# A two-layer decoder step on one core: raw tokens in column pieces as first operands, the norm's factor applied to the projections' outputs, and the samples' sums and recurrence in other steps

## The chip, the core and the metric

The kernel runs on one core of a Trainium2 chip. Five engines work at the same time, each through its own instructions in order: TensorE (PE; its weight loads are shown apart as PEld), VectorE (DVE), ScalarE (ACT), GpSimd (POOL) and SyncE (SP), which here only issues transfers. The metric is the device time of one execution in microseconds (us). Times of before are a median of three runs; the profile is of one further execution.

## The reference

One inference step of a decoder with a prompt of 1024 tokens and 8 single-token samples that share all weights (width 1024, FFN width 2816, fp32). Layer A mixes with a gated linear recurrence (4 heads, a 128x128 state each) beside attention over 256 memory tokens, layer B with stick-breaking attention beside memory attention; each is followed by a SwiGLU FFN. Every sub-layer has a norm before and behind it. What the change touches, in short:

```python
def rmsnorm(x, g):
    y = xf * lax.rsqrt(jnp.mean(xf * xf, axis=-1, keepdims=True) + EPS)
    return (y * g.astype(jnp.float32)).astype(x.dtype)
def a_mixer(hn, w_in, lb, hg_gain, mem_k, mem_v, w_o, s0):      # hn = rmsnorm(h, g[0])
    q_h, f_h, i_h, g_h, q_m = jnp.split(hn @ w_in, 5, axis=-1)
    q = jax.nn.silu(q_h)                       # logf, k from f_h; v = i_h
    o, S = hgrn2_scan(q, k, v, logf, s0)       # S <- exp(logf) * S + k v,  o = q S
    o = rmsnorm(o, hg_gain) * jax.nn.silu(g_h)
    om = mem_attend(q_m, mem_k, mem_v)         # softmax(q k / sqrt(d)) v
    return jnp.concatenate([o, om], axis=-1) @ w_o, S
```

Since `hn @ w_in` is linear, a token's factor 1/rms can be applied to a projection's output as well as to its input.

## The kernel before

The prompt is worked on in two groups of 512 tokens (g = 0 and 1); the 8 samples ride with group 1, whose rows are 520 wide. Activations lie with the features across partitions, eight blocks of 128 (`ND` = 8). Every fp32 operand is split in two fp32r tiles, a high part (a cast on ScalarE) and the remainder (a subtraction on VectorE, `split_to` and the pair L208/L209 for weights), and every product is three matmuls (high by high, high by low, low by high). TensorE therefore has 24 matmuls of 512 columns for a projection of one head (`proj`, L222), and the FFN's gate and up projections are partly done with Strassen's seven products (`gate_up_w`; L571, L573 split its weights, L578 is its product).

**The start.** `start(0)` waits for four blocks of 128 tokens by 1024 features, norms each (`rms_rows`: squares at L331 or L333, Ln and Exp, multiplication L336), turns them feature by feature on TensorE (L363, four transposes for one block of 128 features) and multiplies by the norm's gain while it splits (L366 on ScalarE, L367 on VectorE). The first projection is that of the values, token rows out (`rows_proj`, L1183: for each of eight feature blocks, twelve matmuls in two pairs of banks), whose weights are cast at L1177 and L1178 and whose result is copied at L1189 and L1190. The gate's projection (`gate_proj`) follows, L222 again, then q.

**The samples' recurrence.** `hgrn_sample` goes through four heads: a state tile and the values of one head, copied to all partitions, are fetched one head ahead (L1248, from the input and from `vd`). On VectorE the state is multiplied by F (L1272), the values by K (L1273), they are added (L1274), and stored (L1275); the next step multiplies by Q (L1278) and splits for TensorE. It is woven with the second group's gate projections and with the FFN of group 0.

**The samples' memory attention.** `mem_attn_sample` has `sample_scores` and `sample_pv`, which for each sample loads its cached values, multiplies and adds them on VectorE, splits them, and sums over partitions on TensorE (L1071 into one bank); the result is copied (L1091), turned (L1095) and split. It is woven with the prompt's memory attention (L978 turns the probabilities, L991 multiplies by the values) and with the FFN, first an ordinary part (L504 is Strassen's product in it) and then the part with L571 to L578.

**What sets the order.** The program is written with generators that `weave` mixes: each stream has a weight, and the stream with the smallest count of steps over its weight goes next, so a weight decides between which products a step's instructions fall. `tc.issue_after(split[0].ins)` puts an instruction behind the last weight split. Within an engine the order of instructions is that of the program so laid out. PSUM has three banks with tag `s` (`S()`), one with tag `ns` (`NS()`) and four for products.

## Time and profile before

| | |
|---|---|
| three runs | 2410.87 us median (2408.98 to 2412.88) |
| the profiled execution | 2413.43 us |
| its span, first to last instruction | 2411.6 us, mean clock 0.998 |
| VectorE, ScalarE, by 40 us from 40 to 200 | 28.7, 34.5, 30.1, 19.8 and 27.0, 18.5, 17.3, 25.9 us |
| TensorE in the first 40 us | 29.2 us, later 40.0 of 40 |

Lines of the profile read: start and duration in us, engine, source line, operation, tile written, tiles read, how many; in brackets how long the engine had been idle and what released it. A row with "x84" stands for a run of 84 instructions. Rows of SP with the letter q show when a transfer was issued, not when it landed. A windows row gives the stretch, then each engine's busy time with its count, then the granted clock (1 is full), the share of time the DMA engines were busy, and GB/s.

### The profile page before, as it was taken

The page shows a single profiled execution, that of the slowest core. Times are in us where ns is not written, and L with a number is a line of the kernel's source. Part 1 is how long each engine was busy: PE and PEld are TensorE (multiplying, and loading weights), DVE is VectorE, ACT ScalarE, POOL GpSimd, SP SyncE. Part 2 cuts the span into 40 slices and gives each one's busy share as a digit, 9 for nine tenths or more (in the row PEclk, how much of TensorE's full clock was granted, in tenths as well). Part 3 has the DMA queues.
Part 4 walks back from the last instruction along what each step waited for, and adds up shares of the span by engine and source line. Part 5 has one row for each costly group of instructions (what it writes and reads, how often), then busy time and mean ns, then how long its engine had stood idle before and what let it go on. Part 6 is the DMA issues. An engine that isn't in the chain of part 4 may idle for free.

```text
span 2411.6 us, 42315 instructions
## 1 busy us (share of the span) xinstructions
PE 2379.0 (99%) x15959; PEld 2156.3 (89%) x15959; DVE 1734.8 (72%) x3220; ACT 1283.5 (53%) x2559; POOL 113.2 (5%) x187
## 2 busy tenths in 40 slices
PE   8999999999999999999999999999999999999998
PEld 6888989888789998999999989877778899999998
DVE  5867558666896676879666777778787679776866
ACT  5547544444454554667544554556454466554445
POOL 1000202100000000000001200111000000000000
PEclk9999999999999999999999999999999999999999
DMA  6454766566644447432568846545353354343342
GB/s 189 123 167 111 173 194 163 132 187 181 203 140 136 146 139 217 124 112 81 163 176 218 230 141 190 173 137 157 109 157 118 99 160 136 105 130 100 109 128 76
DMA packets 510991, 357.59 MB, mean 148 GB/s; under 512 B 20109, under 2 KB 459514, under 8 KB 510786
## 3 DMA queue, kind: packets, MB, share of 16 engines
q1 hardware_dynamic: 494914, 312.93, 43.6%
q0 software_dynamic: 15872, 41.95, 7.5%
q8 instruction: 126, 2.06, 0.4%
q14 instruction: 79, 0.65, 0.1%
HBM read 322.86 MB, written 65.49 MB: 161 GB/s over the span
## 4 chain that ended last, share of the span: by engine, by line
PE 51%; DVE 2%; ACT 2%; DMA 1%; issue 1%; DVEq 0%; SPq 0%; ACTq 0%
PE mm L222 17%; PE q L578 16%; PE q L750 10%; PE q L504 1%; PE s L1565 1%; PE s L1525 1%; PE q L782 1%; PE s L1010 1%; PE s L991 1%; PE s L1554 1%; DMA w<-in_w_in_b 0%; DVE x L230 0%; PE ns L1071 0%; PE s L978 0%; PE s L504 0%
## 5 line engine op out<-in xcount | busy, mean ns | idle before, releaser
L222 PE MATMUL mm<-x,ws 128*128 128x512 f32 (+1 forms) x5016 | 925.5, 342 | 5.3 <-DVE ws L209 1.5
L222 PEld LDWEIGHTS mm<-x,ws 128*128 128x128 f32 x5016 | 774.5, 188 | 115.9 <-issue 3.9
L208 ACT CAST ws<-w 128x512 fp32r<-128x512 f32 x596 | 347.9, 585 | 435.5 <-PE mm L222 254.4
L209 DVE TENSOR_TENSOR ws<-w,ws 128x512 fp32r<-128x512 f32 x596 | 380.9, 645 | 227.2 <-ACT ws L208 224.2
L750 PE MATMUL q<-m,ws 128*128 128x260 f32 (+1 forms) x2496 | 304.2, 282 | 0.4 <-DVE m L230 0.2
L750 PEld LDWEIGHTS q<-m,ws 128*128 128x128 f32 x2496 | 299.7, 188 | 1.6 <-ACT m L229 0.7
L578 PE MATMUL q<-y,ws 128*128 128x260 f32 (+1 forms) x1920 | 249.6, 284 | 0.5 <-ACT q L586 0.5
L578 PEld LDWEIGHTS q<-y,ws 128*128 128x128 f32 x1920 | 237.8, 189 | 1.6 <-ACT q L586 0.7
L578 PE MATMUL q<-x,ws 128*128 128x260 f32 (+1 forms) x1668 | 220.4, 283 | 3.0 <-ACT ws L571 1.6
L578 PEld LDWEIGHTS q<-x,ws 128*128 128x128 f32 x1668 | 207.8, 188 | 4.4 <-ACT ws L571 2.2
L222 PE MATMUL mm<-m,ws 128*128 128x512 f32 x768 | 187.2, 397 | 0.0
L571 ACT CAST ws<-w 128x512 fp32r<-128x512 f32 x206 | 125.1, 619 | 96.3 <-PE q L750 30.7
L573 DVE TENSOR_TENSOR ws<-w,ws 128x512 fp32r<-128x512 f32 x206 | 139.5, 688 | 44.7 <-ACT ws L571 43.4
L222 PEld LDWEIGHTS mm<-m,ws 128*128 128x128 f32 x768 | 142.5, 188 | 31.3
L759 DVE TENSOR_TENSOR r<-r,q 128x260 f32<-128x260 f32 (+1 forms) x160 | 60.6, 420 | 48.7 <-PE q L750 48.6
L504 PE MATMUL q<-x,ws 128*128 128x260 f32 (+1 forms) x720 | 87.1, 282 | 0.0
L504 PEld LDWEIGHTS q<-x,ws 128*128 128x128 f32 x720 | 86.4, 188 | 0.2
L229 ACT CAST m<-t 128x512 fp32r<-128x512 f32 (+1 forms) x88 | 54.8, 623 | 49.0 <-DVE t L819 26.9
L571 ACT CAST ws<-b 128x512 fp32r<-128x512 f32 x82 | 50.5, 620 | 39.2 <-PE q L750 13.4
L573 DVE TENSOR_TENSOR ws<-b,ws 128x512 fp32r<-128x512 f32 x82 | 56.4, 688 | 17.8 <-ACT ws L571 15.9
L230 DVE TENSOR_TENSOR m<-t,m 128x512 fp32r<-128x512 f32 (+1 forms) x88 | 60.8, 691 | 11.2 <-ACT m L229 10.4
L277 DVE TENSOR_TENSOR st<-st,n 128x512 f32<-128x512 f32 (+1 forms) x91 | 62.2, 691 | 4.0 <-ACT n L276 2.7
(410 smaller groups left out, 3092.0 us busy)
## 6 DMA issues: line engine op xcount, KB each, us to landing
w<-in_w_gu SPq DMA_DIRECT2D x275, 256.0 KB, 3.3
w<-in_w_down SPq DMA_DIRECT2D x160, 256.0 KB, 3.0
wsum<-in_w_gu POOLq DMA_DIRECT2D x48, 512.0 KB, 6.0
w<-in_w_in_a SPq DMA_DIRECT2D x80, 256.0 KB, 3.0
w<-in_w_o SPq DMA_DIRECT2D x64, 256.0 KB, 3.0
w<-wsum SPq DMA_DIRECT2D x61, 256.0 KB, 3.1
b<-in_w_gu SPq DMA_DIRECT2D x39, 256.0 KB, 4.0
b<-wsum SPq DMA_DIRECT2D x39, 256.0 KB, 3.3
```

Of the source, the lines that this page charges most:

```text
L208: nc.scalar.copy(ws[:, 0, :n, :], raw[:, :n, :])
L209: split[0] = nc.vector.tensor_sub(ws[:, 1, :n, :], raw[:, :n, :], ws[:, 0, :n, :].bitcast(F32))
L222: nc.tensor.matmul(ps[:, a, : PW[g]], wt, xt[k][:, xi, o : o + PW[g]], start=(k == 0 and wi == 0), stop=(k == nk - 1 and wi == 2),)
L229: nc.scalar.copy(dst[0], src)
L230: nc.vector.tensor_sub(dst[1], src, dst[0].bitcast(F32))
L277: nc.vector.tensor_add(acc[:, :n], acc[:, :n], t[:, :n])
L504: ins = nc.tensor.matmul(pp[a][:, :h], wt, xt[k][:, xi, a * h : (a + 1) * h], start=(k == 0 and wi == 0), stop=(k == ND - 1 and wi == 2),)
L571: nc.scalar.copy(w[:, 0, :], src)
L573: split[0] = nc.vector.tensor_sub(w[:, 1, :], src, w[:, 0, :].bitcast(F32))
L578: nc.tensor.matmul(ps[:, :h], w[:, wj, k * P : (k + 1) * P], x[:, xi, :], start=(first and k == 0 and wi == 0), stop=(k == 3 and wi == 2), ...
L750: nc.tensor.matmul(pp[a][:, :h], wt, mids[k][:, xi, a * h : (a + 1) * h], start=(k == 0 and wi == 0), stop=(k == nf - 1 and wi == 2),)
L759: nc.vector.tensor_add(d, d, pp[a][:, :h])
```

## The change

**Start.** The tokens of group 0 come in eight pieces of 128 features by 512 tokens, between them the first five blocks of the values' weights. Only the gains of the norms are loaded before them. Transposes and first operands are made of the raw tokens times the gain; their instructions and the products are tied to alternate (`turned`, `summed`). The factors (`token_scales`) are computed later: squares, Ln, Exp, a diagonal, and a product of ones with it, that lays the 512 factors across all partitions (`rows`). Values get the factor of their token when they are copied out, q, gate and memory query by a multiplication with `rows` on VectorE; for the f gate and the memory query this takes the place of a copy on ScalarE. The masks are cast once instead of seven times.

**Samples.** Some small transposes and sums that used the three banks `s` use the bank `ns`. In the recurrence a step ends behind the multiplication by F, and the two following multiplications stand behind the last weight split. Two weights of `weave` are others: 16 for 12 and 70 for 82.

The diff, cut:

```diff
     xtok = [rpool.tile([P, CH, D], F32, tag="r", name="xtok0")]
-    for tb in range(CH):
-        nc.sync.dma_start(xtok[0][:, tb, :], x_prompt[0, tb * P : (tb + 1) * P, :])
     prow = tpool.tile([P, P], F32, tag="t", name="prow")
-    nc.vector.memset(prow, 0.0)
     nc.sync.dma_start(prow[0:NR, :], g_norm.rearrange("l i (k p) -> (l i k) p", p=P))
-    nc.sync.dma_start(prow[NR : NR + ND, :], g_kv.rearrange("(k p) -> k p", p=P))
-    nc.sync.dma_start(prow[NR + ND : NR + ND + H, :], hg_lb.rearrange("l (h p) -> (l h) p", p=P))
-    nc.sync.dma_start(prow[NR + ND + H : NR + ND + H + 1, :], hg_norm)
+    wfirst = []
+    for k in range(ND):
+        cs = slice(k * P, (k + 1) * P)
+        nc.sync.dma_start(xtok[0][:, :, cs], x_prompt[0, :G, cs].rearrange("(c p) d -> p c d", p=P))
+        if k < 5:
+            wfirst.append(wraw.tile([P, 512], F32, tag="w", name=nm("w")))
+            nc.sync.dma_start(wfirst[k], w_in_a[0][cs, 8 * P : 12 * P])
+    prest = tpool.tile([P, P], F32, tag="t", name="prest")
+    nc.sync.dma_start(prest[0:ND, :], g_kv.rearrange("(k p) -> k p", p=P))
+    nc.sync.dma_start(prest[ND : ND + H, :], hg_lb.rearrange("l (h p) -> (l h) p", p=P))
+    nc.sync.dma_start(prest[ND + H : ND + H + 1, :], hg_norm)
...
-    def silu(dst, ps, g):
+    def silu(dst, ps, g, scale=None):
         n = NG[g]
         x = T()
         dst = T() if dst is None else dst
         d = dst[:, :n]
-        nc.vector.tensor_scalar(sv(x, g), pv(ps, g), -44.0, None, op0=ALU.max)
+        src = pv(ps, g)
+        if scale is not None:
+            nc.vector.tensor_mul(sv(x, g), src, scale)
+            src = sv(x, g)
+        nc.vector.tensor_scalar(sv(x, g), src, -44.0, None, op0=ALU.max)
...
+    def token_scales(out):
+        ss = small([P, 8], tag="rr")
+        for tb in range(CH):
+            xt = xtok[0][:, tb, :]
+            junk = M().rearrange("p a n -> p (a n)")[:, :D]
+            with tc.issue_after(turned[-1][tb % 2]):
+                if tb % 2:
+                    nc.vector.tensor_tensor_reduce(junk, xt, xt, 1.0, 0.0, ALU.mult, ALU.add, ss[:, tb : tb + 1])
+                else:
+                    nc.scalar.activation(junk, xt, AF.Square, accum_out=ss[:, tb : tb + 1])
+        nc.scalar.activation(ss[:, :CH], ss[:, :CH], AF.Ln, scale=1.0 / D, bias=epsb)
+        nc.scalar.activation(ss[:, :CH], ss[:, :CH], AF.Exp, scale=-0.5)
+        d = B()
+        nc.vector.tensor_mul(
+            d.rearrange("p (c t) -> p c t", c=CH), ident.unsqueeze(1).to_broadcast([P, CH, P]),
+            ss[:, :CH].unsqueeze(2).to_broadcast([P, CH, P]),
+        )
+        ps = S()
+        nc.tensor.matmul(ps, ones, d, start=True, stop=True)
+        rows = M()[:, 0, :G]
+        nc.scalar.copy(rows, ps)
+        out.extend((ss, rows))
...
             ps = S() if k % 2 else NS()
-            for tb in range(CH):
-                nc.tensor.transpose(ps[:, tb * P : (tb + 1) * P], xtok[g][:, tb, k * P : (k + 1) * P], ident)
+            with ExitStack() as tied:
+                if summed[0] and not g:
+                    tied.enter_context(tc.issue_after(summed[0].ins))
+                for tb in range(CH):
+                    nc.tensor.transpose(ps[:, tb * P : (tb + 1) * P], xtok[g][:, tb, k * P : (k + 1) * P], ident)
             x = X(g)
             gk = gcol(0, 0, k)
-            nc.scalar.activation(x[:, 0, :G], ps, AF.Copy, scale=gk)
+            raised = nc.scalar.activation(x[:, 0, :G], ps, AF.Copy, scale=gk)
...
+            if not g:
+                turned.append((raised.ins, made[0].ins))
...
-        pq = S()
+        pq = NS()
...
-    def rows_proj(W, m0, xt, dst):
+    def rows_proj(W, m0, xt, dst, raws=(), scale=None):
         pb = [mmp.tile([P, 2, 512], F32, tag="mm", name=nm("mm")) for _ in range(2)]
         for k in range(ND):
-            raw = wraw.tile([P, 512], F32, tag="w", name=nm("w"))
-            nc.sync.dma_start(raw, W[k * P : (k + 1) * P, m0 : m0 + H * P])
+            if k < len(raws):
+                raw = raws[k]
+            else:
+                raw = wraw.tile([P, 512], F32, tag="w", name=nm("w"))
+                nc.sync.dma_start(raw, W[k * P : (k + 1) * P, m0 : m0 + H * P])
             ws = wspl.tile([P, 2, 512], F32R, tag="ws", name=nm("ws"))
-            nc.scalar.copy(ws[:, 0, :], raw)
-            nc.vector.tensor_sub(ws[:, 1, :], raw, ws[:, 0, :].bitcast(F32))
+            with ExitStack() as tied:
+                if raws:
+                    tied.enter_context(tc.issue_after(turned[k][0]))
+                nc.scalar.copy(ws[:, 0, :], raw)
+            with ExitStack() as tied:
+                if raws:
+                    tied.enter_context(tc.issue_after(turned[k][1]))
+                nc.vector.tensor_sub(ws[:, 1, :], raw, ws[:, 0, :].bitcast(F32))
...
+                        summed[0] = nc.tensor.matmul(
...
-            if k % 2:
+            if k % 2 or raws:
                 yield
-        nc.scalar.copy(dst[0][:, :, :512], pb[0])
-        nc.vector.tensor_copy(dst[1][:, :, :512], pb[1])
-    def v_proj(g, W, m0, xt, vt, vs):
+        if scale is None:
+            nc.scalar.copy(dst[0][:, :, :512], pb[0])
+            nc.vector.tensor_copy(dst[1][:, :, :512], pb[1])
+            return
+        for a in range(2):
+            nc.scalar.activation(dst[0][:, a, :512], pb[0][:, a, :], AF.Copy, scale=scale[0][:, a : a + 1])
+            nc.vector.tensor_scalar(dst[1][:, a, :512], pb[1][:, a, :], scale[0][:, 2 + a : 3 + a], None, op0=ALU.mult)
...
             f = T()
-            nc.scalar.copy(sv(f, g), pv(ps, g))
+            if rows is None:
+                nc.scalar.copy(sv(f, g), pv(ps, g))
+            else:
+                nc.vector.tensor_mul(sv(f, g), pv(ps, g), rows)
...
                 nc.vector.tensor_mul(stv, stv, col(Ft))
-            nc.vector.tensor_mul(vbv, vbv, col(Kt))
+            yield
+            with tc.issue_after(split[0].ins):
+                nc.vector.tensor_mul(vbv, vbv, col(Kt))
             nc.vector.tensor_add(st, st, vb)
             nc.sync.dma_start(st_sample[0, :, h].rearrange("b k v -> k b v"), stv)
             total()
             yield
-            nc.vector.tensor_mul(vbv, stv, col(Qt))
+            with tc.issue_after(split[0].ins):
+                nc.vector.tensor_mul(vbv, stv, col(Qt))
...
-    def scaled_evac(dst, ps, g):
+    def scaled_evac(dst, ps, g, rows=None):
+        if rows is not None:
+            nc.vector.scalar_tensor_tensor(sv(dst, g), pv(ps, g), SCALE, rows, op0=ALU.mult, op1=ALU.mult)
+            return
...
+    scales = []
+    a0 = mixer_a(0, x0, scales)
+    v = a0.v()
+    next(head)
+    for _ in range(ND):
+        next(v)
+        next(head, None)
+    token_scales(scales)
+    with tc.issue_after(made[0].ins):
+        columns(prest, NR, ND + H + 1)
+        nc.vector.tensor_copy(selr, sel)
+        nc.vector.tensor_copy(mask, masks)
...
-    drain(head)
-    a0 = mixer_a(0, x0)
-    drain(a0.v())
+    drain(v)
...
-    weave((a1.sample(), 12), (a1.gate(), 4), (f0.part(1), 14), (w0, 9))
+    weave((a1.sample(), 16), (a1.gate(), 4), (f0.part(1), 14), (w0, 9))
...
-    weave((chain(a1.merge(), a1.mem()), 27), (a1.mem_sample(), 82), (rest(), 33))
+    weave((chain(a1.merge(), a1.mem()), 27), (a1.mem_sample(), 70), (rest(), 33))
```

How the instructions move, at three places. On TensorE at the start, first before, from the second block of features on (L363 turns tokens, L1183 are value products):

```order
L363 MATMUL s_254<-ident,xtok_100 128x128 x4
L363 MATMUL s_270<-ident,xtok_100 128x128 x4
L363 MATMUL ns_246<-ident,xtok_100 128x128 x4
L1183 MATMUL mm_296<-ws_300,x_174 128x512 x4
L1183 MATMUL mm_297<-ws_300,x_174 128x512
L363 MATMUL s_286<-ident,xtok_100 128x128 x4
L1183 MATMUL mm_297<-ws_300,x_174 128x512 x2
```

Now (L157 turns the gains, L399 tokens, L1232 are value products):

```order
L157 MATMUL s_139<-ident,prow 128x64
L399 MATMUL ns_159<-ident,xtok_100 128x128 x4
L399 MATMUL s_193<-ident,xtok_100 128x128 x4
L1232 MATMUL mm_203<-ws_205,x_164 128x512 x6
L1232 MATMUL mm_204<-ws_205,x_164 128x512 x6
L399 MATMUL ns_220<-ident,xtok_100 128x128 x4
L1232 MATMUL mm_203<-ws_228,x_198 128x512 x6
L1232 MATMUL mm_204<-ws_228,x_198 128x512 x6
L399 MATMUL s_243<-ident,xtok_100 128x128 x4
```

Products of a block now begin after the transposes of one further block, instead of several. At the end of the values, in the change, ScalarE (L217 casts the gate's weights, L360 and L361 make the factors, L1243 copies out values) and TensorE (L950 turns memory tokens, L368 is the product with the diagonal, L231 the gate's first) have:

```order
L217 CAST ws_435<-w_433 128x512
L217 CAST ws_501<-w_499 128x512
L360 ACTIVATE rr_379<-rr_379,epsb 128x4
L217 CAST ws_506<-w_504 128x512
L361 ACTIVATE rr_379<-rr_379 128x4
L217 CAST ws_550<-w_548 128x512
L1243 ACTIVATE a_201<-mm_203,rr_379 128x512 x2
```

```order
L1232 MATMUL mm_203<-ws_364,x_342 128x512 x6
L1232 MATMUL mm_204<-ws_364,x_342 128x512 x6
L950 MATMUL ns_481<-ident,c_479 128x128 x4
L368 MATMUL s_392<-b_390,ones 128x512
L157 MATMUL s_396<-ident,prest 128x13
L231 MATMUL mm_438<-x_164,ws_430 128x512 x3
```

Two values' copies now stand behind the factors and the cast into `ws_550`, and three pieces of TensorE work ahead of the gate's first product.

On VectorE in the samples' recurrence, before (L209 splits weights, L230 operands, L247 and L819 empty banks):

```order
L230 TENSOR_TENSOR b_5591<-c_5363,b_5590 128x512
L209 TENSOR_TENSOR ws_5599<-w_5597,ws_5599 128x512
L230 TENSOR_TENSOR m_5460<-t_5409,m_5460 128x512
L209 TENSOR_TENSOR ws_5604<-w_5602,ws_5604 128x512
L1272 TENSOR_TENSOR c_5466<-c_5466,a_2494 128x1024
L1273 TENSOR_TENSOR c_5637<-c_5637,a_2495 128x1024
L247 TENSOR_SCALAR t_5537<-mm_5488 128x520
```

And now (L1329 is the multiplication by F, L1332 by K, L218 splits weights, L239 operands, L260 and L859 empty banks):

```order
L264 TENSOR_TENSOR a_5209<-a_5209,t_5528 128x520
L218 TENSOR_TENSOR ws_5641<-w_5639,ws_5641 128x512
L1329 TENSOR_TENSOR c_5464<-c_5464,a_2492 128x1024
L1332 TENSOR_TENSOR c_5465<-c_5465,a_2493 128x1024
L260 TENSOR_SCALAR t_5569<-mm_5544 128x512
L239 TENSOR_TENSOR b_5631<-c_5322,b_5630 128x512
L1333 TENSOR_TENSOR c_5464<-c_5464,c_5465 128x1024
```

The split that last reads the previous head's values (`c_5363`, now `c_5322`) stood five rows ahead of the multiplication by K, with their tile as the place that the next values are fetched into; now it stands behind that multiplication, whose tile `c_5465` was left free 26 rows before.

At the end of the samples' memory attention on TensorE, before (L1071 sums, L1095 last transposes, L578 Strassen's products):

```order
L1071 MATMUL ns_6735<-n_7326,selr 8x512
L1071 MATMUL ns_6735<-b_7327,selr 8x512
L1071 MATMUL ns_6735<-n_7511,selr 8x512
L1071 MATMUL ns_6735<-b_7512,selr 8x512
L978 MATMUL s_7521<-ident,b_7338 128x128 x4
L991 MATMUL s_7528<-b_7349,c_6494 128x256 x2
L1095 MATMUL s_7531<-ident,b_7519 128x8 x4
L578 MATMUL q_7545<-a_7009,ws_7568 128x256 x2
L991 MATMUL s_7528<-b_7526,c_6494 128x256 x2
L578 MATMUL q_7544<-x_3792,ws_7550 128x256 x3
L578 MATMUL q_7544<-x_3860,ws_7550 128x256 x3
```

Now, a good deal of L578 (here L618) later (L1111 sums, L1135 last transposes):

```order
L618 MATMUL q_7507<-a_7391,ws_7597 128x256 x3
L618 MATMUL q_7508<-x_3936,ws_7618 128x256 x3
L618 MATMUL q_7508<-x_4004,ws_7618 128x256 x3
L618 MATMUL q_7508<-x_4011,ws_7618 128x256 x3
L618 MATMUL q_7508<-x_4075,ws_7618 128x256 x3
L1111 MATMUL ns_6794<-n_7638,selr 8x512
L1111 MATMUL ns_6794<-b_7639,selr 8x512
L1135 MATMUL ns_7671<-ident,b_7646 128x8 x4
L618 MATMUL q_7507<-a_6986,ws_7650 128x256 x2
```

And on SP, in the change (L1144 loads cached values, L578 tiles for the products L618, L212 weights):

```order
L1144 DMA c_7544<-in_cache_mem_v 128x2x512
L212 DMA w_7750<-in_w_down 128x4x128
L1144 DMA c_7634<-in_cache_mem_v 128x2x512
L578 DMA b_7558<-wsum_2365 128x4x128
L578 DMA b_7595<-wsum_2366 128x4x128
L212 DMA w_7783<-in_w_down 128x4x128
L212 DMA w_7816<-in_w_down 128x4x128
L578 DMA b_7648<-in_w_gu 128x4x128
L578 DMA b_7970<-wsum_3667 128x4x128
L578 DMA b_8005<-in_w_gu 128x4x128
```

The last sums and transposes have moved from ahead of those products to between them, and on SP the loads of the last samples' cached values now stand among, and ahead of, the tiles for the products; `c_7634` there waits for a product, the twelfth with `ws_7511`.

More of the change, by code (lines that the diff above doesn't have):

```diff
@@ L148, in tile_decoder, with columns @@
     par = const.tile([P, P], F32, name="par")
-    pp = S()
-    nc.tensor.transpose(pp[:, :P], prow, ident)
-    nc.scalar.copy(par, pp[:, :P])
+    def columns(t, o, n):
+        pp = S()
+        nc.tensor.transpose(pp[:, :n], t[:n, :], ident[:n, :n])
+        nc.scalar.copy(par[:, o : o + n], pp[:, :n])
+    columns(prow, 0, NR)
     def gcol(l, i, k):
@@ L346, in start @@
             nc.sync.dma_start(xs, x_sample.rearrange("b o d -> (b o) d"))
-        for tb in range(CH):
-            rms_rows(xtok[g][:, tb, :], P, g == 0 and tb % 2 == 1)
-            yield
         if g:
+            for tb in range(CH):
+                rms_rows(xtok[g][:, tb, :], P)
+                yield
             ps = S()
@@ L1204, in v_proj, with gate_proj @@
             yield
-    def gate_proj(g, W, xt, Ft, Kt):
+    def gate_proj(g, W, xt, Ft, Kt, rows):
         n = NG[g]
@@ L1674, in tile_decoder @@
     head = start(0, x0)
-    while not made[0]:
-        next(head)
+    next(head)
     with tc.issue_after(made[0].ins):
@@ L1709, in tile_decoder @@
             )
[L1710 removed]
+    scales = []
+    a0 = mixer_a(0, x0, scales)
+    v = a0.v()
+    next(head)
+    for _ in range(ND):
[6 more added lines that the diff above has]
+        nc.vector.tensor_copy(mask, masks)
         lb = const.tile([P, H], F32, name="lb")
```

44 lines of the change are left out of this document (22 added, 22 removed).

## Prediction

> **What bounds the kernel now.** I read the page's busy shares first, then the waits of TensorE, since only they tell what an engine that is nearly always busy still loses.
>
> ```profile
> PE 2379.0 (99%) x15959; PEld 2156.3 (89%) x15959; DVE 1734.8 (72%) x3220; ACT 1283.5 (53%) x2559; POOL 113.2 (5%) x187
> PE ns L363 <- DVE xtok L336: 10.2, 2, 7.9
> PE q L578 <- ACT ws L571: 1.8, 3, 1.3
> PE mm L222 <- DVE t L819: 1.5, 1, 1.5
> PE mm L222 <- DVE t L247: 1.2, 1, 1.2
> ```
>
> TensorE is busy for all but 32 us of the 2411.6 us span, and its work is not made less: no product is taken away. So the change can win only where TensorE waits or runs at half its clock, and it loses wherever it puts a new wait into a stream that has almost none. Three places matter: the start (10.2 us of waits in one group), two stalls of 1.5 and 1.2 us, and the stretch around L578.
>
> The start by stages, in a table of windows (engine busy times, granted clock, DMA share), and then row by row in the timeline:
>
> ```profile
> 0.00:5.00 5.00, 0.00 (x0) 0.00 (x0) 0.63 (x4) 1.75 (x2) 3.74 (x15) 1.00 0.64 212
> 5.00:10.00 5.00, 0.92 (x2) 0.36 (x2) 3.31 (x5) 3.33 (x10) 0.00 (x0) 1.00 0.78 270
> 10.00:15.00 5.00, 3.77 (x20) 3.59 (x20) 3.41 (x12) 3.17 (x8) 1.93 (x7) 1.00 0.89 295
> ...
> 0.79 1.81 SPq L131 DMA_DIRECT2D xtok<-in_x_prompt  x4
> 2.65 0.65 SPq L134 DMA_DIRECT2D prow<-in_g_norm  x1
> 4.54 1.06 ACT L333 ACTIVATE m<-xtok 128x1024 f32<-128x1024 f32 x1 [2.46 <-DMA xtok<-in_x_prompt]
> 11.23 0.48 PE L363 MATMUL ns<-ident,xtok 128*128 128x128 f32 x1 [2.29 <-DVE xtok L336]
> 12.19 2.55 PE L363 MATMUL s<-ident,xtok 128*128 128x128 f32 x11
> 12.49 0.69 ACT L366 ACTIVATE x<-ns,par 128x512 fp32r<-128x512 f32 x1 [0.26 <-PE ns L363]
> 14.53 0.69 PE L363 MATMUL ns<-ident,xtok 128*128 128x128 f32 x4
> 20.09 19.71 PE L1183 MATMUL mm<-ws,x 128*128 128x512 f32 x84
> 38.43 1.01 ACT L1189 COPY a<-mm 128x1024 f32<-128x1024 f32 x1 [0.78 <-PE mm L1183]
> 39.63 5.73 PE L222 MATMUL mm<-x,ws 128*128 128x512 f32 x24
> ```
>
> The first 512 KB of tokens are there at 4.54, 3.3 us after their issue; then four norms in a row, and the transposes in earnest only from 11.23. From 20.09 the value products run without a gap, 19.71/84 = 0.235 us each, and the gate projection follows at 39.63, before the last values are copied away. Eleven transposes take (14.53−12.19)/11 = 0.213 us each, the next four about 0.11: TensorE starts at half rate and is at full rate some 3.4 us after it got busy.
>
> **Part 1, the start.** The norms go from in front of the transposes to behind them; a first operand needs one 256 KB piece, four transposes, and one pass on ScalarE and VectorE.
>
> ```profile
> w<-in_w_in_a SPq DMA_DIRECT2D x80, 256.0 KB, 3.0
> b<-wsum SPq DMA_DIRECT2D x39, 256.0 KB, 3.3
> ```
>
> Two issues (0.65, and 1.81/4 = 0.45) from 0.79 end at 1.9; a 256 KB load takes 3.0 (4.9); four transposes at half rate 0.85 (5.75); the raise 0.69 with its 0.26 of waiting (6.7): first product at 6.8. From there 96 products are 22.5, and the six batches of four transposes that are left, at 0.44, are 2.6: the values end at 31.9. The handover is new: on ScalarE a weight cast waits for the last value product ahead of the two scaled evacuations, so that the gate's bank comes free after three operations of some 0.62, with their releases 2.6 later, of which the memory's transposes and the product of ones and diagonal cover about half. The gate starts at 34.5. Before, it was 39.63, plus 0.44 for the memory's transposes that now lie ahead: 40.07. That is −5.6. Half rate for 3.4 us, which the old kernel spent largely on transposes, now falls on products and costs half of it, 1.7: −3.9. I take **−3.5**, since a piece or a cast will be late somewhere; bounds −5.6 (full rate from the first product) and −1.5 (a second such period, and 0.7 of late casts).
>
> [...]
>
> **Part 2, the factor on the outputs.** Sixteen evacuations (four gates, four q, four sg, four qm) get a multiply on VectorE, or move there from ScalarE.
>
> ```profile
> 46.08 0.69 DVE L1216 SCALAR_TENSOR_TENSOR t<-t 128x512 f32<-128x512 f32 x1 [2.11 <-ACT t L1214]
> 50.00:60.00 10.00, 10.00 (x45) 8.14 (x44) 7.45 (x14) 7.68 (x14) 0.00 (x0) 1.00 0.28 81
> ```
>
> 16×0.69 = 11.0 us more for VectorE, one per projection of 24×0.235 = 5.6 us. In 50 to 60 it has 2.55 us of 10 free, and needs 1.4 more. It is covered there: I take **+0.3** for single late casts. Bounds 0 and, without cover, half of the 11: +5.5.
>
> **Part 3, the samples' recurrence.** L1273 on VectorE waits for the values' load:
>
> ```profile
>   DMA c<-vd: 11.6, 3
> ...
> 528.62 1.23 DVE L1273 TENSOR_TENSOR c<-c,a 128x1024 f32<-128x1024 f32 x1 [3.77 <-DMA c<-vd]
> 530.59 5.79 PE L222 MATMUL mm<-x,ws 128*128 128x512 f32 x24 [1.48 <-DVE t L819]
> 540.45 0.37 SPq L1248 DMA_DIRECT2D c<-vd  x1
> 547.79 1.23 DVE L1273 TENSOR_TENSOR c<-c,a 128x1024 f32<-128x1024 f32 x1 [4.43 <-DMA c<-vd]
> ```
>
> VectorE is in order, so a bank evacuation (L819, L247) stands behind that wait and TensorE behind it: 1.48 and 1.18. The load lands 7.3 us after its issue (540.45 to 547.79). In the change's order the load of a head's values goes into the buffer that the head two before has left, and 20 or more VectorE rows of about 0.7 us lie between that and the product: 14 us against 7.3, so both stalls go. **−2.7**; bounds −3.0 and 0 (if a wait returns elsewhere).
>
> **Part 4, the tail of the samples' memory.** The weight 82→70 moves the last sample values from ahead of L578's first products to between them.
>
> ```profile
> 742.29 0.68 DVE L1091 COPY b<-ns 8x512 f32<-8x512 f32 x1 [0.30 <-PE ns L1071]
> 742.83 0.46 SPq L538 DMA_DIRECT2D b<-in_w_gu  x1
> 743.49 0.41 PE L1095 MATMUL s<-ident,b 8*128 8x8 f32 x4
> 743.93 0.17 ACT L229 CAST x<-s 128x8 fp32r<-128x8 f32 x1 [0.56 <-PE s L1095]
> 744.93 0.17 DVE L230 TENSOR_TENSOR x<-s,x 128x8 fp32r<-128x8 f32 x1 [0.23 <-ACT x L229]
> 745.77 0.63 ACT L571 CAST ws<-b 128x512 fp32r<-128x512 f32 x1
> 746.46 0.50 PE L578 MATMUL q<-x,ws 128*128 128x256 f32 x2 [1.26 <-ACT ws L571]
> 747.27 1.45 PE L578 MATMUL q<-x,ws 128*128 128x256 f32 x10 [0.31 <-DVE ws L573]
> 755.51 1.58 PE L578 MATMUL q<-x,ws 128*128 128x256 f32 x12
> ...
> 742.00:746.00 4.00, 3.19 (x20) 2.24 (x18) 1.93 (x6) 2.47 (x8) 0.00 (x0) 1.00 0.73 205
> 746.00:750.00 4.00, 3.23 (x19) 3.03 (x20) 4.00 (x8) 4.00 (x9) 0.00 (x0) 0.82 0.73 193
> 750.00:754.00 4.00, 4.00 (x28) 4.00 (x28) 2.33 (x5) 1.84 (x4) 0.00 (x0) 0.75 0.96 279
> ```
>
> Even before, this handover lost 1.58 us, and the clock then fell: 0.18 and 0.25 of 4 us, another 1.7. The change keeps this and adds. On SP, as the order above shows, a load of cached values now waits for the twelfth product of q, and behind it are queued two b tiles from wsum and the next down weights. The first b tile is issued 0.4+0.46 after that wait, lands 3.3 later and is cast in 0.63: 4.8. Meanwhile TensorE has twelve products of 0.118 (twelve in 755.51 to 756.93) and two of 0.24: 1.9. That leaves a stall of 2.9. Later the last transposes (L1135) stand directly behind the sums (L1111), and the copy between them (0.68, which two groups of products covered before) costs 0.8; the four pairs of small splits behind it (743.93 to 745.10, 1.2) and the cast after them keep the next product some 2.1. Sum +5.8, and +7.5 if the clock falls a second time. Against that stands that a stall gives the next load time, and that the cached values' load may be released early: 0 at the least. I take **+4.0**, nearer the upper end, since each link is a row.
>
> The other samples' sums that go from three banks to the single one keep their neighbours in the order, so they add nothing; a wait of one evacuation (0.7) at some of them is inside the range.
>
> **Sum:** −3.5 + 0.3 − 2.7 + 4.0 = −1.9. It is made against the span of 2411.6; that execution took 2413.43, inside the 2408.98 to 2412.88 of the timed runs but for 0.55, so I put the difference on their median, 2410.87: **2409.0**.
>
> **Rivals.**
>
> *The tail is hidden.* The first b tile comes early enough, as the loads that were issued at 742.83 and 743.59 did for the following products. For it: in the old tail only the first cast cost over 1 us. Against: the wait on SP is ahead of the b tiles in the order. Then −3.5−2.7+0.3 = −5.9, with a tail of +1 at most and the start up to −5: 2403 to 2406, say 2404.5.
>
> *The tail costs what its chain says, and the clock falls again.* Place: L1111 to L1135, price +7.5; the start with a longer cold period, −2.3. It decides when the tail costs over 6.4. For it: 1.58 us lost in about 4 us sufficed for half rate at 748. Then −2.3−2.7+0.3+7.5 = +2.8: 2413.7, up to 2416. [...]
>
> *VectorE becomes the bound under the gates and q.* Half of the 11 us comes out: +5.5 instead of +0.3, 2414.2. Against it: 1.4 us needed where 2.55 are free.
>
> **How the numbers follow.** Forecast 0.45 (own range 2406 to 2412), hidden tail 0.27, full tail 0.18, VectorE 0.10. A difference below 0.2% (4.8 us) I count as no change, about what these runs can tell: faster means below 2406.05, slower above 2415.7. Faster: 0.08 of the forecast's share, 0.27 of the hidden tail's: 0.35. Slower: 0.02, 0.11 and 0.06: 0.19. The rest, 0.46. The range 2402.5 to 2416 takes in the first three but for their ends and half of the fourth; about 0.15 is left out.
>
> **What would show it.** Start: first value product near 7, gate's first product at 34 to 37 (right), beyond 38.5 (wrong). Recurrence: no wait of VectorE for the values' load, no stall over 1 us of L222 there. Tail: TensorE idle between L1111 and L1135 of 3 to 6 us in all with a clock below 1; if it is below 1 us, the hidden tail is right. Under the gates, TensorE must stay at 10.0 of 10 from 40 to 100. I am wrong if a wait appears in a stage not named here.

## The result, and the profile after

The change is slower: 2418.08 us, median of 11 runs (2414.32 to 2421.22), against 2412.40 of 11 runs of the kernel before. The ratio is 1.0021, with an interval of 1.0013 to 1.0030: +5.1 us. The profiled execution took 2415.38 us with a span of 2413.7, one of the fastest of the eleven; its span is only 2.1 us above that of before. Both numbers need an explanation. One of twelve later runs of the change (e9) took 3331.55 us at a mean granted clock of 0.654 and is in no ratio.

From the page of the change, and from its waits of TensorE (line waited for, us in total, times, longest):

```profile
PE 2382.3 (99%) x15962; PEld 2160.4 (90%) x15962; DVE 1738.8 (72%) x3227; ACT 1275.4 (53%) x2548; POOL 114.1 (5%) x187
PE q L618 <- ACT ws L611: 6.8, 5, 3.1
PE s L157 <- DMA prow<-in_g_norm: 3.1, 1, 3.1
```

The 10.2 us that TensorE waited for normed tokens are gone, and so are the two stalls behind L819 and L247. The first row of the waits is new in size: 6.8 us for casts of L618's tiles, where the same products (L578) waited 1.8 before.

**The start** of the change, TensorE's rows of its timeline:

```profile
4.58 1.12 PE L399 MATMUL ns<-ident,xtok 128*128 128x128 f32 x4 [1.13 <-DMA xtok<-in_x_prompt]
6.54 1.12 PE L399 MATMUL s<-ident,xtok 128*128 128x128 f32 x4 [0.84 <-DMA xtok<-in_x_prompt]
7.30 4.39 PE L1232 MATMUL mm<-ws,x 128*128 128x512 f32 x12
...
11.88 3.01 PE L1232 MATMUL mm<-ws,x 128*128 128x512 f32 x12
...
27.94 5.83 PE L1232 MATMUL mm<-ws,x 128*128 128x512 f32 x24
33.61 0.60 PE L950 MATMUL ns<-ident,c 128*128 128x128 f32 x4
35.02 1.13 PE L368 MATMUL s<-b,ones 128*128 128x512 f32 x2 [0.81 <-DVE b L363]
36.08 0.23 PE L157 MATMUL s<-ident,prest 13*128 13x13 f32 x1
36.24 5.83 PE L231 MATMUL mm<-x,ws 128*128 128x512 f32 x24
```

The first piece lands at 4.6, the second 2 us later, and the first value product runs at 7.30. Its twelve take 4.39 us, the next twelve 3.01, so TensorE ran at half rate for a part of them. (The granted clock of the windows reads 1.00 in these first microseconds; the half rate shows in the durations alone: 0.24 us from one product to the next in the second twelve, 0.35 in the first.) The values' last product ends at 33.7, and the gate starts 2.5 us behind it, at 36.24 against 40.07 (39.63 and the 0.44 of the memory's transposes). What fills these 2.5 us is in the rows: the memory's transposes, a wait of 0.81 for the diagonal (L363), its product and a last small transpose. The copies of the values on ScalarE (L1243), for whose bank the prediction had the gate wait, ended at 35.6, and no wait stands in front of the gate's first product.

**The recurrence.** The view of the multiplication by K shows no idle time in front of it (before: 11.6 us in three waits):

```profile
L1332 DVE TENSOR_TENSOR c<-c,a x4: 1218/1218/1222, 507.1 to 564.9; 128x1024 f32<-128x1024 f32 x4
its engine sat idle before it (us, times) until:
who waited for it (us, times):
```

**The tail of the samples' memory**, timeline of the change:

```profile
740.62 0.37 SPq L1144 DMA_DIRECT2D c<-in_cache_mem_v  x1
741.09 0.96 SPq L578 DMA_DIRECT2D b<-wsum  x2
...
742.93 0.40 PE L1111 MATMUL ns<-b,selr 128*8 128x512 f32 x1 [0.33 <-DVE b L239]
745.79 0.62 ACT L611 CAST ws<-b 128x512 fp32r<-128x512 f32 x1 [3.64 <-DMA b<-wsum]
...
746.46 0.50 PE L618 MATMUL q<-a,ws 128*128 128x256 f32 x2 [3.13 <-ACT ws L611]
...
754.28 0.40 PE L1111 MATMUL ns<-b,selr 128*8 128x512 f32 x1
...
754.71 0.68 DVE L1131 COPY b<-ns 8x512 f32<-8x512 f32 x1
...
755.45 0.41 PE L1135 MATMUL ns<-ident,b 8*128 8x8 f32 x4 [0.77 <-DVE b L1131]
...
757.14 0.62 ACT L611 CAST ws<-b 128x512 fp32r<-128x512 f32 x1
...
757.82 0.80 PE L618 MATMUL q<-a,ws 128*128 128x256 f32 x2 [1.96 <-ACT ws L611]
```

This is the chain of the prediction, link by link. The b tile is issued behind the cached values' load at 741.09, is cast at 745.79, and TensorE waits 3.13 us; the copy between sums and transposes costs 0.77; the small splits and the cast behind them 1.96. In the windows of the same stretch (in the order: before, change):

```profile
740.00:760.00 20.00, 18.43 (x131) 16.81 (x130) 12.64 (x26) 11.14 (x25) 0.00 (x0) 0.91 0.79 222
760.00:780.00 20.00, 20.00 (x172) 20.00 (x171) 12.08 (x25) 6.11 (x10) 0.00 (x0) 1.00 0.45 129
```

```profile
720.00:740.00 20.00, 18.50 (x136) 16.74 (x136) 12.85 (x30) 11.36 (x23) 0.00 (x0) 1.00 0.16 52
740.00:760.00 20.00, 13.33 (x81) 11.63 (x79) 11.81 (x22) 7.59 (x19) 0.00 (x0) 0.86 0.60 172
760.00:780.00 20.00, 20.00 (x165) 20.00 (x165) 12.23 (x25) 6.90 (x12) 0.00 (x0) 0.97 0.61 171
```

TensorE's busy time falls from 18.43 to 13.33 (the 1.5 us that before loses here lie in 720 to 740 now), and the granted clock, which had been short by 0.09 of 20 us (1.8 us, one period of some 3.4 us at half rate: 0.79, 0.50, 0.50 and 0.50 in the single microseconds from 748 to 752), is now short by 0.14 and 0.03: 3.4 us, two such periods (0.79, 0.50, 0.50, 0.51 from 747 to 751, and 0.91, 0.50, 0.50, 0.50, 0.89 from 757 to 762). The first product of Strassen's part and the start of the down projection (L750, now L790) tell the sum, before and then in the change:

```profile
743.83 0.51 PE L578 MATMUL q<-a,ws 128*128 128x256 f32 x2
...
758.34 3.83 PE L750 MATMUL q<-m,ws 128*128 128x256 f32 x31
```

```profile
735.18 0.59 PE L618 MATMUL q<-a,ws 128*128 128x256 f32 x2
...
758.41 0.72 PE L790 MATMUL q<-m,ws 128*128 128x256 f32 x2
758.93 2.34 PE L618 MATMUL q<-a,ws 128*128 128x256 f32 x10
761.07 3.21 PE L790 MATMUL q<-m,ws 128*128 128x256 f32 x25
```

The change enters the stretch 8.6 us ahead (some 2 us of that because sums and transposes have moved into it). It leaves it more than 2 us behind: at 758.41 it has ten of Strassen's products still to do, and only two of the down projection done when they end at 761.07.

### The profile page after: what moved, and what is told of

The parts are those of the page before. It is cut to its first block, busy times and chain, and to the rows that moved or that the text cites. A ratio compares the mean times of both kernels' runs of the same rounds, so it can differ in the third digit from the quotient of the medians.

```text
span 2413.7 us, 42324 instructions
## 1 busy us (share of the span) xinstructions
PE 2382.3 (99%) x15962; PEld 2160.4 (90%) x15962; DVE 1738.8 (72%) x3227; ACT 1275.4 (53%) x2548; POOL 114.1 (5%) x187
## 4 chain that ended last, share of the span: by engine, by line
PE 50%; DVE 2%; ACT 2%; DMA 1%; issue 1%; DVEq 0%; SPq 0%; ACTq 0%
PE mm L231 16%; PE q L618 16%; PE q L790 10%; PE q L544 1%; PE s L1631 1%; PE q L822 1%; PE s L1591 1%; DMA b<-qd 1%; PE s L1050 1%; PE s L1031 1%; PE s L1620 0%; DMA w<-in_w_in_b 0%; DVE ws L218 0%; DVE x L239 0%; PE ns L1111 0%
## 5 line engine op out<-in xcount | busy, mean ns | idle before, releaser
L231 PE MATMUL mm<-x,ws 128*128 128x512 f32 (+1 forms) x5016 | 924.7, 342 | 2.2 <-ACT a L1467 1.1
L231 PEld LDWEIGHTS mm<-x,ws 128*128 128x128 f32 x5016 | 774.9, 188 | 111.7 <-DVE ws L218 2.1
L217 ACT CAST ws<-w 128x512 fp32r<-128x512 f32 x596 | 347.4, 585 | 434.2 <-PE mm L231 265.3
L218 DVE TENSOR_TENSOR ws<-w,ws 128x512 fp32r<-128x512 f32 x596 | 381.3, 645 | 235.0 <-ACT ws L217 230.2
L790 PE MATMUL q<-m,ws 128*128 128x260 f32 (+1 forms) x2496 | 305.1, 283 | 0.4 <-ACT m L238 0.2
L790 PEld LDWEIGHTS q<-m,ws 128*128 128x128 f32 x2496 | 300.5, 189 | 1.6 <-ACT m L238 0.7
L618 PE MATMUL q<-y,ws 128*128 128x260 f32 (+1 forms) x1920 | 249.6, 284 | 0.4 <-ACT q L626 0.4
L618 PEld LDWEIGHTS q<-y,ws 128*128 128x128 f32 x1920 | 237.8, 189 | 1.5 <-ACT q L626 0.6
L618 PE MATMUL q<-x,ws 128*128 128x260 f32 (+1 forms) x1668 | 221.4, 284 | 3.0 <-ACT ws L611 1.6
L618 PEld LDWEIGHTS q<-x,ws 128*128 128x128 f32 x1668 | 208.8, 189 | 4.3 <-ACT ws L611 2.2
L231 PE MATMUL mm<-m,ws 128*128 128x512 f32 x768 | 186.7, 397 | 0.0
L231 PEld LDWEIGHTS mm<-m,ws 128*128 128x128 f32 x768 | 142.9, 188 | 31.6 <-DVE m L239 0.2
L239 DVE TENSOR_TENSOR m<-t,m 128x512 fp32r<-128x512 f32 (+1 forms) x88 | 60.8, 691 | 12.0 <-ACT m L238 11.1
```

The costliest lines, as they stand in the source:

```text
L217: nc.scalar.copy(ws[:, 0, :n, :], raw[:, :n, :])
L218: split[0] = nc.vector.tensor_sub(ws[:, 1, :n, :], raw[:, :n, :], ws[:, 0, :n, :].bitcast(F32))
L231: nc.tensor.matmul(ps[:, a, : PW[g]], wt, xt[k][:, xi, o : o + PW[g]], start=(k == 0 and wi == 0), stop=(k == nk - 1 and wi == 2),)
L239: nc.vector.tensor_sub(dst[1], src, dst[0].bitcast(F32))
L618: nc.tensor.matmul(ps[:, :h], w[:, wj, k * P : (k + 1) * P], x[:, xi, :], start=(first and k == 0 and wi == 0), stop=(k == 3 and wi == 2), ...
L790: nc.tensor.matmul(pp[a][:, :h], wt, mids[k][:, xi, a * h : (a + 1) * h], start=(k == 0 and wi == 0), stop=(k == nf - 1 and wi == 2),)
```

## The experiments

Ratios are to the kernel before, with their interval; each group of four ran on one chip. A part was put into the kernel before, or taken out of the change.

| | ratio | interval |
|---|---|---|
| the change | 1.0021 | 1.0013 to 1.0030 |
| the change again (e9) | 1.0022 | 1.0013 to 1.0030 |
| before against itself (e5) | 1.0001 | 0.9992 to 1.0010 |
| before + weight 70 (e2) | 1.0052 | 1.0039 to 1.0065 |
| before + start and factor (e3) | 0.9993 | 0.9984 to 1.0001 |
| before + recurrence, weight 16 (e4) | 1.0005 | 0.9997 to 1.0014 |
| the same again (e6) | 0.9999 | 0.9990 to 1.0008 |
| change, weight 82 (e1) | 0.9981 | 0.9973 to 0.9990 |
| change, weight 82, old banks (e12) | 0.9974 | 0.9964 to 0.9984 |
| change, weight 82, TensorE kept busy first (e8) | 0.9990 | 0.9981 to 0.9999 |
| change, paced scores, weight 95 (e10) | 0.9981 | 0.9973 to 0.9990 |
| the same, TensorE kept busy first (e11) | 0.9982 | 0.9974 to 0.9991 |

### The weight, taken out of the change and put into the kernel before

```diff
-    weave((chain(a1.merge(), a1.mem()), 27), (a1.mem_sample(), 70), (rest(), 33))
+    weave((chain(a1.merge(), a1.mem()), 27), (a1.mem_sample(), 82), (rest(), 33))
```

> The change, with the samples' memory attention back at weight 82 (nothing else undone). Theory 'tail': the stretch from the last sample values to the first down products lost 13.9 us of TensorE's time in the profile of the change against 5.4 before, and that goes back to 5.4; start and recurrence keep their gains, so about 2406 to 2408, 0.997 to 0.9985 of before. Rival 'displaced': the other edits push the same waits to another place whatever the weight, so the time stays within 2 us of the change's 2418.

```diff
-    weave((chain(a1.merge(), a1.mem()), 27), (a1.mem_sample(), 82), (rest(), 33))
+    weave((chain(a1.merge(), a1.mem()), 27), (a1.mem_sample(), 70), (rest(), 33))
```

> The kernel before with the weight 70 alone. Theory 'tail': +7 to +9 us, ratio 1.003 to 1.004, with TensorE waiting some 3 us for a b tile and some 2 us behind the last transposes, and half clock twice. Rival 'displaced': the weight alone does nothing in the old order, within 2 us of before.

One number turns the change from +5.1 us to −4.6: 9.7 us, to within some 3 us, since each ratio has an interval of 0.0009 either way. In the old kernel the same number costs 12.5 us (9.4 to 15.7), more than was expected. Its waits of TensorE and the windows of the old kernel with weight 70:

```profile
PE q L578 <- ACT ws L571: 6.5, 5, 2.8
```

```profile
740.00:760.00 20.00, 14.40 (x89) 11.82 (x87) 11.89 (x18) 6.92 (x15) 0.00 (x0) 0.91 0.53 150
760.00:780.00 20.00, 18.03 (x131) 17.95 (x130) 11.78 (x25) 9.17 (x19) 0.00 (x0) 0.83 0.54 154
```

The same kind of waits (2.77, 0.77 and 1.97 in its timeline), and 5.2 us of clock (0.09 and 0.17 of 20). "Displaced" is refuted: the cause is the weight, and it needs none of the other edits.

### Start and recurrence alone

e3 is the change with the old recurrence, the old banks and the weights 12 and 82. e4 is the kernel before with:

```diff
-            nc.vector.tensor_mul(vbv, vbv, col(Kt))
+            yield
+            with tc.issue_after(split[0].ins):
+                nc.vector.tensor_mul(vbv, vbv, col(Kt))
...
-            nc.vector.tensor_mul(vbv, stv, col(Qt))
+            with tc.issue_after(split[0].ins):
+                nc.vector.tensor_mul(vbv, stv, col(Qt))
...
-    weave((a1.sample(), 12), (a1.gate(), 4), (f0.part(1), 14), (w0, 9))
+    weave((a1.sample(), 16), (a1.gate(), 4), (f0.part(1), 14), (w0, 9))
```

> The kernel before with the new start and the factor on the outputs alone (old banks, old recurrence, weights 12 and 82). Theory: -3.5 to -4 us, ratio near 0.9985, the gate's first product at 36.2. Rival 'given back': VectorE's 11 us more lets casts come late between 40 and 230 and takes back 2 us or more, ratio 0.9993 or above.

> The kernel before with the recurrence in three steps and weight 16 alone. Theory: both stalls of TensorE near 529 and 548 go, -2.7 to -3.2 us, ratio near 0.9988. Rival: the wait moves to another place of the same stretch, within 1 us of before.

The start's 0.9993 is −1.7 us (−3.9 to +0.2): less than expected, though not surely so, and the number of the rival. But nothing is given back where the rival puts it: from 40 to 500 us TensorE is busy for 459.84 of 460 us, as before (459.88). In this profile the gate starts only at 37.45, and near 636 TensorE waits 1.80 us for a weight split (L218), followed by 1.6 us of lost clock (0.92 from 620 to 640). The recurrence did not gain: +1.2 us (−0.7 to +3.4), although its profile shows both stalls gone. So it was run again, beside the kernel before against itself.

> The kernel before, unchanged, against itself: how far two sets of runs of one program lie apart, and whether the stalls near 638 and 1360 us (0.6 and none in its first profile, 2.3 and 2.2 in that of the recurrence alone) belong to the program or to the execution. Theory 'execution': the ratio is 1.000 within 0.001, and the stalls differ from the first profile's by 1 us or more. Rival 'program': the same stalls within 0.3 us.

> The recurrence alone once more. Theory: what it gains up to 755 us (3 us in its profile) is there in every execution, and its timed +1.2 was made by later stalls that come and go, so the ratio now is 0.9985 to 1.000. Rival: it loses again, 1.0005 or more, with the stall of over 2 us near 637 there again: then the wait was moved to the samples' scores.

The kernel before against itself gives 1.0001, as the theory of e5 had it. The stalls it named, though, are those of the first profile (0.39 for 0.46 near 637, nothing near 1360), as its rival said. The stall near 1360 that the first profile of the recurrence shows (2.1 us, and 1.6 of clock) is absent in e6, so that one belongs to an execution.

The recurrence came out at 0.9999, so with the first run it is worth nothing that can be told. The two second profiles show one place near 637 us where it gives time back. The kernel before (e5):

```profile
635.20 1.22 DVE L1057 TENSOR_TENSOR c<-c,b 128x1024 f32<-128x1024 f32 x1
...
636.34 0.69 DVE L209 TENSOR_TENSOR ws<-w,ws 128x512 fp32r<-128x512 f32 x1
...
637.08 4.20 PE L222 MATMUL mm<-x,ws 128*128 128x512 f32 x17 [0.39 <-DVE ws L209]
```

The recurrence alone (e6):

```profile
635.92 1.21 DVE L1060 TENSOR_REDUCE sc<-c 128x8 f32<-128x1024 f32 x1
637.04 1.22 DVE L1057 TENSOR_TENSOR c<-c,b 128x1024 f32<-128x1024 f32 x1
...
638.78 0.68 DVE L209 TENSOR_TENSOR ws<-w,ws 128x512 fp32r<-128x512 f32 x1
639.52 1.66 PE L222 MATMUL mm<-x,ws 128*128 128x512 f32 x6 [1.70 <-DVE ws L209]
```

The recurrence with its weight shifts what follows: here the weight split L209 stands behind one more pair of the samples' scores (L1060, L1057, 1.2 us each) and two gate operations (L247, L251, 0.7 each) than in the old order, and TensorE waits 1.70 for it (2.12 in e4) instead of 0.39 (0.46 in the first profile of before). The first stall's 1.5 and, where it occurs, the second's 1.2 go, and 1.3 to 1.7 come back 100 us later. That the order alone does this is not shown: e3, with the old recurrence and the old order at this place, waits 1.80 there as well. The second stall, by L247, is absent from the second profile of before: it was an execution's, not the program's. That second profile has a span of 2408.0 against 2411.6, and this window:

```profile
740.00:760.00 20.00, 18.43 (x144) 17.03 (x142) 14.23 (x29) 11.66 (x26) 0.00 (x0) 1.00 0.86 236
```

The stalls of the tail are the same as in the first profile (18.43), but the clock does not fall: the 1.8 us of the first profile belong to its execution. The other profiles say the same. Eleven in all have this tail (weight 82, or 95 paced, with 18.43), and the clock fell in three of them (0.91 in before, e1 and e7; 1.00 in the others).

### The change again, and its clock

> The change once more. Theory 'tail': in a second profile the three waits behind L1111 and L1135 are again about 3.1, 0.8 and 2.0 us, with half clock after them, and no stall near 635; the ratio is again 1.001 to 1.003. Rival 'execution': these waits vary by 1 us or more as those near 1360 did, and the ratio falls to 1.000.

```profile
740.00:760.00 20.00, 12.88 (x78) 11.15 (x77) 10.87 (x21) 6.20 (x16) 0.00 (x0) 0.81 0.60 170
760.00:780.00 20.00, 20.00 (x160) 20.00 (x161) 12.29 (x25) 8.11 (x15) 0.00 (x0) 0.93 0.59 167
```

The ratio repeats, and so do the waits:

```profile
PE q L618 <- ACT ws L611: 7.5, 5, 3.8
```

The longest is 3.8 instead of 3.1. The granted clock is short by 5.2 us here (0.19 and 0.07 of 20), as much as three periods of 1.7, against 3.4 in the first profile. Some 1.0 of the 5.2 is estimated to have fallen into the waits, where TensorE had nothing to do, and to have cost nothing: the windows from 720 to 780 count 374 products for 382, some 0.9 us less at 0.118 each, in 0.45 us less busy time, so at least 0.5 of the further 1.8 fell on products. So the first two profiles compared a long execution of before with a short one of the change. By spans, the second pair differs by 2417.4 − 2408.0 = 9.4, the first by 2.1; the mean, 5.8, is near the timed 5.1.

The same two pairs give an estimate of the tail. From 720 to 780, TensorE's busy time is 6.6 and 7.0 us less than before (51.84 and 51.39 against 58.43), and the clock takes 1.6 and some 4.2 us more: 8.2 and 11.2, in the mean 9.7. By this estimate the tail alone accounts for what the weight costs.

### Other paces, banks, and the clock at the start

> The change with weight 82 once more, for a second profile. Theory: the gate's first product between 36 and 38, stalls of 1.5 and 0.5 at the tail and none of the kinds that wait for b tiles there, span 2407 to 2410. Rival: a span above 2411.

This run, whose label is wrong, has the change's banks; it was run once, so it has no ratio. Its span is 2408.1, the gate starts at 38.08, and the waits at the tail are those of before: the theory but for 0.1 us of the gate.

e8 and e11 put 14 products of `ones` by `ones` in the queue of TensorE, 8 in front of the gains' transpose and 6 behind it:

```diff
+    hot = mmp.tile([P, 2, 512], F32, tag="mm", name="hot")
+    def heat(n):
+        for _ in range(n):
+            nc.tensor.matmul(hot[:, 0, :P], ones, ones, start=True, stop=True)
+    heat(8)
     columns(prow, 0, NR)
+    heat(6)
```

> The change with weight 82, and 14 products of ones by ones (128 columns, not used) on TensorE before and behind the gains' transpose, from about 1.3 us. Theory 'clock': TensorE is at full rate from the first or second value products on, the first value products are 0.23 apart and not 0.43, the gate starts 1 to 2 us sooner than with weight 82 alone: ratio to before 0.997 to 0.998. Rival: the pieces of tokens set the start, so that products at full rate only wait longer for them: no gain over weight 82 alone.

```profile
1.11 4.77 PE L164 MATMUL hot<-ones 128*128 128x128 f32 x28 [1.11 <-DVE epsb L151]
5.82 0.27 PE L157 MATMUL s<-ident,prow 64*128 64x64 f32 x1
6.02 0.66 PE L407 MATMUL ns<-ident,xtok 128*128 128x128 f32 x4
6.84 0.66 PE L407 MATMUL s<-ident,xtok 128*128 128x128 f32 x4 [0.17 <-DMA xtok<-in_x_prompt]
8.79 1.43 PE L1240 MATMUL mm<-ws,x 128*128 128x512 f32 x5 [1.28 <-ACT ws L1231]
```

(The trace has two records for each of the 14 products.) The transposes take 0.66 instead of 1.12, and the value products run at full rate at once: the first five take 1.43 us, where the first ten took 4.62 in e1. But the unused products last until 5.8, so the tokens' transposes come 1.4 us later than with the change and the first value product at 8.8 instead of 7.2 to 8.4. The gate starts at 36.37, inside the 36.24 to 38.08 of the runs without them, and 0.9990 is no better than the 0.9981 of weight 82 alone. So the rival's number is right, but not its reason: the burst itself is the delay here, and not the pieces. A shorter burst was not tried.

e10 paces the samples' memory attention in two parts:

```diff
+    def paced(steps, n, every):
+        for i, _ in enumerate(steps):
+            yield
+            if i < n and i % every == every - 1:
+                yield
-    weave((chain(a1.merge(), a1.mem()), 27), (a1.mem_sample(), 70), (rest(), 33))
+    weave((chain(a1.merge(), a1.mem()), 27), (paced(a1.mem_sample(), 18, 3), 95), (rest(), 33))
```

> The change, with the samples' memory attention at weight 95 and an empty step behind every third of its first 18 steps, so that the scores go at about the pace of weight 70 and the values end where weight 82 ends them. Theory 'two places': weight 70 takes VectorE's crowding near 635 away (2 us of TensorE there in the recurrence alone, none in the change) and pays at the tail; with both paces right, both go: 2 us less than weight 82, ratio near 0.997. Rival: faster values crowd VectorE under the next products; no better than weight 82 (0.998 to 0.999).

> The same, with the 14 unused products at the start. Theory: another 1 to 2 us, ratio 0.996 to 0.997. Rival: no better than without them.

Near 635 the stall shrank to 0.4 in the profile of e10 (1.0 to 2.0 in four profiles with weight 82), but 0.6 appeared near 668, and the ratios are those of weight 82. The rival's number is right; that crowding of VectorE is the reason rests on one profile.

> The change with weight 82, and the samples' transposes and sums in the three banks again. Theory: the banks are worth nothing here, ratio within 0.001 of weight 82 with the new banks (0.998). Rival: they keep TensorE from waiting for a bank, and without them it is 2 us slower, 0.999 or more, with new waits of TensorE at L1031, L1018 or L618.

With the old banks the change at weight 82 stands at 0.9974, no worse than with the new ones. The banks are worth nothing here that can be told, as the theory said. All five versions of the change without weight 70 beat the kernel before; e12 is the lowest, 2408.40 against 2413.58 on its chip.

## Why the prediction was wrong

**The step that failed** is the price of the tail in part 4: "I take +4.0". The chain there gave 5.8 for its three links, and the trace has 3.13, 0.77 and 1.96 for the 2.9, 0.8 and 2.1 of the text, 5.86 in all. The sign that the text gave for it, 3 to 6 us of idle time between L1111 and L1135 with the clock below 1, was seen too; it was the price that was too small. The clock's second period, put at 1.7, came too (3.4 us in all), and in the second profile as much as a third (5.2). The reason given for taking less (a stall gives the next load time) does not hold here: the three waits have nearly their full size in both profiles of the change. The rows say why. The first wait is for a load behind another on SP, the last for a cast on ScalarE behind splits that cannot start before the transposes, so the earlier stall does not shorten the later one.

The weight is worth 9.7 us in the change (1.0021 and again 1.0022, against 0.9981), where the text had 4.0 and 7.5 as the upper bound of its term. Parts 1 to 3 together, the change at weight 82, gave −4.6 where −5.9 was taken. So of the 7.0 us between −1.9 and +5.1, part 4 has 5.7 and the others 1.3. Most of the rest of the way from 2409.0 to 2418.08 is the base: the three runs of the prediction gave 2410.87, the eleven beside the change 2412.40.

That the first link came out at 3.13 for 2.9 is partly luck. From the release of SP to the end of the cast it took 5.8 us (740.6 to 746.4) and not 4.8, and TensorE had 2.7 us of products meanwhile (to 743.3) and not 1.9.

**The rival** "the tail costs what its chain says, and the clock falls again" is what happened. That its 2413.7 is also the span of the first profile is chance: it was a figure for the median, which is 4 us above it and outside the range. Its upper bound was too low for two reasons. The sum set out from one execution of before whose tail had a period of half rate that most others do not have, so that the change's loss of clock was counted from too high a base; and the two clusters of waits were followed by two periods in one profile of the change (3.4 us) and by as much as three in the other (5.2). Its −2.3, for a start with a longer cold period, was the author's estimate and stands in no row of before; the seven profiles with the new start gave −3.8 to −2.0, in the mean −2.8, and half rate lasted longer in e1 and e3 than in the change (ten products in 4.62 and 4.42 us, against twelve in 4.39).

**Part 1**: the direction was right, the size somewhat large. The gate started 3.8 us sooner in the first pair of profiles (3.5 taken) and 2.6 sooner in the second (37.13 against 39.27 and 0.44). Over the seven profiles with the new start and without unused products it started at 36.24 to 38.08, in the mean 37.2, over the five of the old start at 39.6 and 0.44: 2.8 sooner. Two steps of its working failed. "First product at 6.8" was 7.2 to 8.4, since the second transposes, which stand ahead of the first product, waited for their piece until 6.4 to 7.6; the page of the change has 6.5 us from issue to landing for these 256 KB pieces (median), where the sum took the 3.0 of the weights. And the handover of 2.5 for 2.6 was right in size by luck: the sum had the gate wait for a bank behind three operations of ScalarE, while in the trace TensorE waits for the diagonal, and those operations end 0.6 us before the gate starts. Half rate falling on products held (4.39 us for the first twelve, 3.01 for the next). Alone, the part timed −1.7.

**Part 2** was right that the work is covered: TensorE stays at full share under the gates and q. The 11 us were too many: VectorE's busy time from 40 to 240 us rose from 145.6 to 152.1, by 6.5. Two windows of the change:

```profile
40.00:60.00 20.00, 20.00 (x90) 16.27 (x90) 15.13 (x26) 10.93 (x20) 0.00 (x0) 1.00 0.61 180
...
100.00:140.00 40.00, 40.00 (x317) 37.88 (x317) 34.66 (x94) 13.89 (x28) 0.00 (x0) 1.00 0.55 169
```

**Part 3** was right about the stalls and wrong about the sum: −2.7 counted one stall that only some executions have, and no term stood for a wait later in the stream. Alone it is worth nothing that can be told. In the change the stall near 635 is 0.2 (0.25 in e9) instead of 1.0 to 2.0 with weight 82, so the slower pace of the scores takes most of it away: an advantage of weight 70 that is small beside the tail.

**What stays open.** With weight 82 the parts together give 0.9974 to 0.9981, alone 0.9993 and about 1.0002. The difference, some 4 us, is not much more than the intervals allow, and which parts help each other is open. Whether SP's order or the place of the last transposes is the larger part of the tail was not tried separately; the trace gives 3.1 and 2.7 us, and lost clock behind both. Why the weight costs 12.5 us in the old kernel and 9.7 in the change is open too, though the intervals overlap.

What makes the clock fall is open as well. The same stalls at the tail's entry cost 1.8 us of clock in three profiles and none in eight, so the 1.58 us lost there, which the rival took to suffice for half rate, do not settle it. In the profile of before that the prediction rests on, the clock fell although TensorE was busy for 3.19 and 3.23 of 4 us from 742 to 750.

## What to carry to other kernels

When each link of a chain has been read from a row and nothing runs beside it, take the whole chain as the forecast, not a part of it. Where two profiles of one program differ by more than the effect (3.6 us here), single spans decide nothing: time in pairs, and use profiles only for where. A weight that sets the pace of a side stream has to be checked at its end, where its last steps fall into the next stage, and not only where it crowded.

## What the runs showed of the hardware

The same stalls are not always followed by half rate. Eleven profiles have the same entry into the tail (18.43 of 20 us busy from 740 to 760). In three of them the granted clock there is 0.91, one period of some 3.4 us at half rate; in eight it is 1.00. The two clusters of waits that weight 70 makes were followed by two such periods in the first profile of the change (3.4 us of clock), and by as much as three in its second and in the old kernel with that weight (5.2 each). So the granted clock was short by 0 to 1.8 us with the one order and by 3.4 to 5.2 us with the other, and one profile alone does not tell which. What decides between the executions was not tried.
